# One encoder layer in fp32 on one core: attention sums kept as channels x tokens up to the output projection, with the group norms applied to partial products

## The chip, the core and the metric

The kernel runs on one core of a Trainium2 chip. The core has a matrix engine (TensorE; PE in the profile, with its weight loads as PEld), a vector engine (VectorE, DVE), a scalar engine (ScalarE, ACT), a general engine (GpSimd, POOL) and a queue for transfers (SyncE, SP). Each engine works through its own instructions in order, and semaphores make one wait for another. On-chip memory (SBUF) has 128 partitions; TensorE writes its results to PSUM, eight banks of 128 x 512 fp32 numbers. The metric is the time of one execution on the device in microseconds (us).

## What is computed

One layer of an encoder for 1024 tokens of 1024 channels, all in fp32 (cut from the reference):

```python
hn = rms_norm(x, norm1_g)
proj = hn @ w_in                       # 1024 x 2304: qA kA vA qB kB vB
qa = axial_rope(rms_norm(qa)); ka = axial_rope(rms_norm(ka))
out_a = softmax(qa @ ka.T / 8) @ va    # 8 query heads, 2 key/value heads, head size 64
out_b = mixture of three dilated windows with ALiBi, merged by their softmax denominators   # 8 heads
mixed = concat([rms_norm(out_a, outa_norm_g), rms_norm(out_b, outb_norm_g)])   # two groups of 512
x = x + mixed @ w_out
x = x + conv_ffn(rms_norm(x, norm2_g)) # up 1024 -> 5632, width-3 conv, gelu gate, down 2816 -> 1024
```

`rms_norm` of a group divides each token's 512 channels by the root of their mean square and multiplies them by a gain.

## The kernel before

**Numbers.** A product of two fp32 matrices is made from three faster products of "high" and "low" parts (tiles in `bigr`): high x high, high x low, low x high. For each operand ScalarE copies the high part and VectorE (sometimes GpSimd) subtracts it from the original to give the low part. Products in plain fp32 (`f(...)` operands) take two passes.

**Stages, in order of time.** (1) The input projection, by a seven-product (Strassen-like) scheme, with the queries, keys and values prepared in its wake; to about 200 us. (2) Mixer A, to 391 us: 16 groups, one for each pair of a 128-token query block `b` and a key/value head `kv`; a group has four query heads x 128 tokens in its 512 columns. For each of eight key tiles `a_main` (line 924) makes 128 keys x 512 queries of scores in a bank, ScalarE takes the exponential twice (once as the high part, once in place in PSUM), VectorE subtracts to give the low part, and three steps later `pv` (line 932) multiplies with the values. The values carry a block of 64 columns of ones, so that the denominators come out under the 64 channels: the bank `ob` (6 or 7, by turns) ends with 64 rows of channels and 64 rows that all hold the denominator. `a_prep` (line 895), spread among these steps, prepares the next group, with eight row maxima on VectorE. (3) Mixer B, to about 541 us: eight heads in eight steps each (`b_s`, `b_prep`, `b_pv`, lines 1073, 1009, 1111), the products with the values two steps behind the scores (`lag = 2`, line 1399). Four steps use high and low parts, four use plain fp32 products with the values `F_VCN`, 65 columns wide (64 channels, one of ones). (4) The output projection, to about 645 us. (5) The up-projection with convolution and gate, to about 1055 us. (6) The down-projection to the end.

**From sums to the projection.** In both mixers the sums lie as channels x tokens when they are done. The kernel turns them: `o_turn` (line 942) in A and `b_out` (line 1135) in B make four PE transposes of 65 rows (64 channels and the denominator), and `o_norm` (line 965) takes the reciprocal of four denominators per partition and multiplies. The result lies as tokens x channels at `q_at(...)`. Then, for each of the eight token tiles and two channel groups, `mix_norm` (line 1165) makes the group norm (square and sum on ScalarE, a root, five small VectorE steps, a pass of 512 with the gain), `mix_tr` (line 1174) turns the tile back with four 128-wide PE transposes and splits it into high and low parts from PSUM, and `proj_out` (line 1183) multiplies with the high and low parts of `w_out` (`wo_split`, line 1145). Both channel groups of a tile accumulate in one bank; `h2_a` (line 1197) adds `x` from there and makes the second norm, `h2_b` (line 1213) turns and splits the result for the up-projection.

**Banks and queues.** Scores, transposes and row maxima take banks in turn from one ring of six (`bank_rings(range(6))`), and from two rings of two in the last head of B and in the projection.

**The order of the work.** The program is recorded first. `Recorder` (lines 126 to 448) finds the dependences, gives each instruction a price (`price`, line 273), simulates the five engines (`simulate`, line 316; PE keeps the order as written, the other engines take what is ready with the earliest due time), and `emit` (line 439) writes the instructions out in the order found. So a price or a delay (`LAG`, line 128) in the planner changes the order on DVE, ACT and POOL and nothing else. In the profile every instruction stands under the one line 447.

**The start.** SyncE and ScalarE issue the first loads (lines 840 to 852): columns 0 to 264 of `w_kv` (8 columns of gain and the first of eight blocks of key/value weights), the first 256 columns of `xt` tile 0, and then the rest. `x_prep` (line 566) splits `xt`, `kv_split` (line 599) scales and splits the weights, `kv_proj` (line 610) is the first work on PE.

Of the kernel before, what the change touches and what calls it, by code (L numbers as in the profile page):

```python
# [123 lines left out]

class Recorder:
# [147 lines left out]
    def price(self, op, outs, ins):  # L273
# [42 lines left out]
    def simulate(self, order=None, window=400):  # L316
# [134 lines left out]
def tile_encoder_layer(ctx, tc, x, xt, w_kv, w_in, gains, outg, norm2_g, w_out, w_up, conv,  # L451
# [472 lines left out]
    def a_main(g, prep, tail, late, plan, late_plan):  # L924
# [14 lines left out]
        def o_out():  # L939
            act(f(F_OT[g % 2], 512)[0:65], bank(ob)[0:65], AF.Copy)  # L940

        def o_turn():
# [20 lines left out]
        return [lambda: pv(5), lambda: pv(6), lambda: pv(7), o_out, o_turn]  # L963

    def o_norm(t, step, dst, dims):
        rec = f(SM_T + 88 + 8 * (t % 2), 4)
        vec.reciprocal(rec, pp(512 * t + 64, [step, 4]))
# [818 lines left out]
```

## Time and profile before

| | |
|---|---|
| median of 3 runs | 1274.68 us (1273.49 to 1274.68) |
| the profiled execution | 1274.05 us |
| its span, first to last instruction | 1272.3 us |
| ScalarE busy in the span | 744.6 us (59%) |
| GpSimd busy in the span | 90.8 us (7%) |
| granted TensorE clock | 1.000 |
| moved by DMA | 157.43 MB |

How to read what follows. The page gives each engine's busy time and a row of 40 digits, one for each fortieth of the span (31.8 us): the busy share in tenths, 9 for 90% and more. The chain that ended last is followed back from the last instruction to whatever released it. A group of instructions stands as: engine, operation, what is written from what (`ps` is PSUM, `bigf` and `bigr` the two arrays in SBUF, with partitions x elements), its count, then its busy time in us and the mean length of one in ns, then the engine's idle time just before them and what ended it. Lengths of neighbours on an engine can overlap, so the busy time of a group can be less than count x mean. The timeline has the start and length of a run of like instructions in us. The view by stretches gives, for A:B in us, the length, and each engine's busy time with its number of instructions.

### The profile page before, as it was taken

Reading aid. Unit: us, or ns where it says so; the run is one execution under the profiler, and the core shown is the slowest. Engines: PE = TensorE matmul, PEld = TensorE weight load, DVE = VectorE, ACT = ScalarE, POOL = GpSimd, SP = SyncE. Lnnn points to the kernel's source line nnn. Section 1 sums busy time; section 2 is a strip of 40 time slices with the busy share of each in tenths; the row PEclk is TensorE's granted clock in tenths of the full one; section 3 lists DMA queues with packets and bytes.
Section 4 is the critical chain, followed back from the end, with each engine's and each line's share of the span. In section 5 each row is a group of like instructions: output and inputs, shape, how many; then the busy total and the mean of one; then the engine's idle time right before and its main releaser. Section 6 shows DMA issues by size and latency. Waiting matters only on the chain.

```text
span 1272.3 us, 17870 instructions
## 1 busy us (share of the span) xinstructions
PE 1258.9 (99%) x6244; PEld 1047.8 (82%) x6244; DVE 1078.3 (85%) x1943; ACT 744.6 (59%) x1221; POOL 90.8 (7%) x92
## 2 busy tenths in 40 slices
PE   8999999999999999999999999999999999999998
PEld 7888877888888998878888888888888888888887
DVE  6998899999887887886699999999999998876664
ACT  7875569988887677763455444444444455343331
POOL 0021230010001221001120000000000000000000
PEclk9999999999999999999999999999999999999999
DMA  9251350000004455342312322223322247967872
GB/s 353 90 164 50 83 145 17 18 1 10 1 18 135 116 121 130 123 151 100 108 59 74 112 105 99 90 103 114 116 104 95 96 161 262 351 224 225 292 228 105
DMA packets 118921, 157.43 MB, mean 124 GB/s; under 512 B 50736, under 2 KB 76336, under 8 KB 117808
## 3 DMA queue, kind: packets, MB, share of 16 engines
q1 hardware_dynamic: 117536, 153.02, 37.2%
q0 software_dynamic: 1152, 3.15, 0.9%
q8 instruction: 49, 0.80, 0.3%
q14 instruction: 40, 0.33, 0.1%
q10 hardware_dynamic: 144, 0.14, 0.0%
HBM read 118.26 MB, written 33.82 MB: 120 GB/s over the span
## 4 chain that ended last, share of the span: by engine, by line
PE 96%; DVE 2%; ACT 1%; DMA 1%; issue 0%; POOL 0%; SPq 0%; ACTq 0%; DVEq 0%
PE ps L447 96%; DVE bigf L447 1%; DVE bigr L447 1%; ACT bigr L447 0%; DMA bigf<-xt 0%; DMA bigf<-w_out 0%; ACT L447 0%; ACT ps L447 0%; POOL bigf L447 0%; ACT bigf L447 0%; SPq L447 0%; ACTq L447 0%; DVEq L447 0%
## 5 line engine op out<-in xcount | busy, mean ns | idle before, releaser
L447 PE MATMUL ps<-bigr 128*128 128x512 f32 (+3 forms) x5860 | 1228.3, 369 | 8.3 <-ACT bigr L447 5.4
L447 PEld LDWEIGHTS ps<-bigr 128*128 128x128 f32 x5860 | 1009.8, 186 | 205.8 <-ACT bigr L447 11.0
L447 ACT ACTIVATE bigr<-bigf 128x512 fp32r<-128x512 f32 (+2 forms) x387 | 277.1, 728 | 355.2 <-PE ps L447 300.0
L447 DVE TENSOR_TENSOR bigr<-bigf,bigr 128x512 fp32r<-128x512 f32 (+2 forms) x355 | 284.7, 812 | 56.5 <-ACT bigr L447 54.8
L447 DVE TENSOR_TENSOR bigf<-bigf 128x512 f32<-128x512 f32 (+3 forms) x308 | 212.6, 712 | 22.1 <-DMA bigf<-w_down 13.1
L447 ACT ACTIVATE bigr<-ps 128x512 fp32r<-128x512 f32 (+1 forms) x292 | 166.4, 602 | 79.5 <-PE ps L447 76.9
L447 DVE TENSOR_TENSOR bigf<-ps,bigf 128x512 f32<-128x512 f32 (+3 forms) x260 | 174.4, 680 | 34.7 <-PE ps L447 30.1
L447 DVE SCALAR_TENSOR_TENSOR bigf<-bigf 128x255 f32<-128x255 f32 (+5 forms) x283 | 165.4, 595 | 21.1 <-ACT bigf L447 18.0
L447 ACT ACTIVATE bigf<-bigf 128x1024 f32<-128x1024 f32 (+5 forms) x194 | 152.1, 804 | 36.1 <-DVE bigf L447 30.4
L447 DVE TENSOR_TENSOR bigr<-ps,bigr 128x512 fp32r<-128x512 f32 x188 | 127.1, 684 | 33.9 <-ACT ps L447 23.9
L447 ACT ACTIVATE ps<-ps 128x512 f32<-128x512 f32 x192 | 115.2, 601 | 9.7 <-PE ps L447 8.9
L447 ACT ACTIVATE bigf<-ps 128x512 f32<-128x512 f32 (+3 forms) x112 | 70.3, 634 | 24.0 <-PE ps L447 12.9
L447 DVE TENSOR_REDUCE bigf<-ps 128x1 f32<-128x512 f32 x128 | 81.2, 680 | 0.8 <-PE ps L447 0.7
L447 POOL TENSOR_TENSOR bigr<-bigf,bigr 128x512 fp32r<-128x512 f32 x32 | 41.9, 1313 | 320.6 <-ACT bigr L447 187.7
L447 PE MATMUL ps<-bigf 128*128 128x128 f32 (+2 forms) x384 | 63.2, 294 | 1.0 <-DVE bigf L447 0.8
L447 PEld LDWEIGHTS ps<-bigf 128*128 128x128 f32 (+2 forms) x384 | 43.2, 139 | 14.3 <-DVE bigf L447 2.3
L447 POOL TENSOR_TENSOR bigf<-bigf 128x256 f32<-128x256 f32 (+2 forms) x29 | 36.2, 1269 | 184.2 <-DVE bigf L447 90.2
L447 DVE CUSTOM_DVE_ANT_1 bigf<-ps,bigf 128x432 bf16<-128x432 f32 x64 | 38.6, 603 | 3.4 <-PE ps L447 3.2
L447 DVE CUSTOM_DVE_ANT_0 bigf<-ps,bigf 128x256 bf16<-128x256 f32 x64 | 26.8, 419 | 2.3 <-PE ps L447 1.3
L447 DVE TENSOR_REDUCE bigf<-bigf 128x16 f32<-128x1024 f32 x13 | 15.8, 1215 | 1.1 <-ACT bigf L447 1.1
L447 ACT ACT_TABLE_LOAD x11 | 14.1, 1283 | 4.0 <-DVE bigf L447 2.6
L447 POOL MEMSET bigr<- 64x512 f32 (+2 forms) x18 | 8.2, 477 | 49.5 <-PE ps L447 49.4
(17 smaller groups left out, 51.8 us busy)
## 6 DMA issues: line engine op xcount, KB each, us to landing
bigf<-w_down SPq DMA_DIRECT2D x99, 256.0 KB, 3.8
bigf<-w_up SPq DMA_DIRECT2D x44, 512.0 KB, 3.4
bigf<-gscr SPq DMA_DIRECT2D x77, 256.0 KB, 4.0
gscr<-bigf SPq DMA_DIRECT2D x33, 512.0 KB, 3.2
bigf<-w_in SPq DMA_DIRECT2D x8, 1024.0 KB, 7.1
bigf<-x SPq DMA_DIRECT2D x16, 512.0 KB, 4.5
bigf<-tmx SPq DMA_DIRECT2D x8, 672.0 KB, 4.1
bigr<-bigr SPq DMA_DIRECT2D x16, 256.0 KB, 3.1
```

Source lines behind the costliest of these rows:

```text
L447: method(*args, **kw)
```

## The change

- **No turning.** The values of B (`F_VCN`) get 64 columns of ones, so that B too ends with 64 rows of denominators. `o_out` in A and `b_out` in B take the reciprocal of these rows (256 elements twice per group in A, 512 for each half head in B) and multiply. The result stays channels x tokens, two heads one under the other in a tile of 128 partitions. `o_turn`, `o_norm`, `mix_norm` and `mix_tr` go.
- **Norms.** Squares are summed over channels: GpSimd (and in the last head ScalarE and VectorE) squares the results and adds them up in `F_SS`; `square_sums` turns these sums with four PE transposes for each half of the tokens and group, and VectorE adds over the partitions' remaining 128 channels. `mix_rms` makes all eight tiles' roots of a group at once. The gain is multiplied into `w_out` in `wo_split`. Each channel group now has a bank of its own in the projection; `proj_add` scales it by the token's root and adds it to `x`.
- **Low parts.** In A the low parts of key tiles 0 and 4 are made by GpSimd; the second exponential goes to SBUF for these.
- **Start.** The first loads are twice as wide (rows of 2 KB); tile 3 of `xt` also comes in halves and joins the first half products.
- **Planner.** Some prices and delays change; `MOVES` is empty and adds nothing.

The diff, cut to its core:

```diff
-    LAG = ((215, 200, 200, 200, 195), (150, 150, 140, 185, 157), (135, 122, 140, 168, 115), (150, 150, 150, 150, 80))
+    LAG = ((215, 200, 200, 200, 195), (166, 150, 146, 185, 157), (142, 124, 140, 168, 115), (150, 150, 150, 150, 80))
...
+            t = n / 1.2 + (52 if ps(ins[0]) else 94) + (37 if ps(outs[0]) else 0)
...
+                t += 12
+            if name == "reciprocal":
+                t += 24
...
+            late_weights = 105 if e == 0 and c[0] < 200 and t > free[0] + 20 else 0
+            free[e] = t + c[0] + late_weights
...
-    act_dma(f(F_WC - 8, 264), w_kv[:, 0:264])
-    dma(f(qab(0), 256), xt[0][:, 0:256])
-    kv_load(1, 2)
+    act_dma(f(F_WC - 8, 520), w_kv[:, 0:520])
+    dma(f(qab(0) + 0, 512), xt[0][:, 0:512])
     kv_load(2, 4)
...
         def o_out():
-            act(f(F_OT[g % 2], 512)[0:65], bank(ob)[0:65], AF.Copy)
-
-        def o_turn():
-            t = next_tr()
-            for i in range(4):
-                pe.transpose(bank(t, 65, 128 * i), f(F_OT[g % 2] + 128 * i, 128)[0:65], f(O_IDF, 65)[0:65])
-            o_norm(t, 128, q_at(1, b, kv), ([64, 4], [1, 64]))
+            o, d = F_OT[g % 2], F_OT[g % 2] + 256
+            for u in range(2):
+                rows = slice(64 * u, 64 * u + 64)
+                ps = pp(512 * ob + 128 * u, [256, 2], [1, 128])
+                act(fp(o, [128, 2], [1, 128])[rows], ps[0:64], AF.Copy)
+                vec.reciprocal(fp(d, [128, 2], [1, 128])[rows], ps[64:128])
+            gp.tensor_tensor(f(q_at(1, b, kv), 256), f(o, 256), f(d, 256), op=OP.mult)
+            if kv:
+                o = fp(q_at(1, b, 0), [512, 2], [1, 256])
+                gp.tensor_tensor(heads(f(F_SQ, 512), 2), o, o, op=OP.mult)
+                gp.tensor_tensor(f(F_SQ, 256), f(F_SQ, 256), f(F_SQ + 256, 256), op=OP.add)
+                gp.tensor_tensor(f(F_SS + 128 * b, 128), f(F_SQ, 128), f(F_SQ + 128, 128), op=OP.add)
...
-            act(bank(st), bank(st), AF.Exp)
-            vec.tensor_tensor(r(pl, 512), bank(st), rf(ph, 512), op=OP.subtract)
+            if kt in (0, 4):
+                act(f(p, 512), bank(st), AF.Exp)
+                gp.tensor_tensor(r(pl, 512), f(p, 512), rf(ph, 512), op=OP.subtract)
+            else:
+                act(bank(st), bank(st), AF.Exp)
+                vec.tensor_tensor(r(pl, 512), bank(st), rf(ph, 512), op=OP.subtract)
...
+    def square_sums(u, hf):
+        t = next_tr()
+        for i in range(4):
+            tr_f(t, i, f(F_SS + 512 * hf + 128 * i, 128))
+        vec.tensor_reduce(f(F_RMS + 8 * u + 4 * hf, 4), heads(bank(t), 4), axis=AX.X, op=OP.add)
...
-                mm(bank(6 + rr // 2, 256, 256 * (rr % 2))[0:65], f(F_VCN + 66 * (2 * rr + 1 - u), 65),
+                mm(bank(6 + rr // 2, 256, 256 * (rr % 2)), f(F_VCN + 128 * (2 * rr + 1 - u), 128),
...
-            o = f(F_OS + 512 * hf, 512)
-            vec.tensor_tensor(o[0:65], bank(6 + hf)[0:65], o[0:65], op=OP.add)
+            vec.tensor_tensor(f(F_OD, 512), bank(6 + hf), f(F_OS + 512 * hf, 512), op=OP.add)
+            b_out(h, hf)
 
     def b_out(h, hf):
-        t = next_tr()
-        for i in range(4):
-            pe.transpose(bank(t, 65, 128 * i), f(F_OS + 512 * hf + 128 * i, 128)[0:65], f(O_IDF, 65)[0:65])
-        o_norm(t, 128, q_at(0, 4 * hf, h // 4) + 64 * (h % 4), ([1024, 4], [1, 64]))
+        o, d = f(F_OD, 512), f(F_RD, 512)
+        x = fp(q_at(0, 4 * hf, h // 4) + 128 * (h % 4 // 2), [1024, 4], [1, 128])
+        vec.reciprocal(d[0:64], o[64:128])
+        if h % 2 == 0:
+            gp.tensor_tensor(x[0:64], heads(o[0:64], 4), heads(d[0:64], 4), op=OP.mult)
+            return
+        vec.tensor_tensor(x[64:128], heads(o[0:64], 4), heads(d[0:64], 4), op=OP.mult)
+        sq, ss = f(F_SQ, 512), f(F_SS + 512 * hf, 512)
+        if h == 1:
+            gp.tensor_tensor(heads(ss, 4), x, x, op=OP.mult)
+        elif h < 7:
+            gp.tensor_tensor(heads(sq, 4), x, x, op=OP.mult)
+            gp.tensor_tensor(ss, ss, sq, op=OP.add)
+        else:
+            act(heads(sq, 4), x, AF.Square)
+            vec.tensor_tensor(ss, ss, sq, op=OP.add)
...
+    def mix_rms(u):
+        s, v, rt, t = [f(F_RMS + 16 * i + 8 * u, 8) for i in range(4)]
+        vec.tensor_scalar(v, s, 1.0 / 512, EPS, op0=OP.mult, op1=OP.add)
+        act(rt, v, AF.Sqrt)
+        newton(s, v, rt, t)
+
+    def mix_split(i, u):
+        o, d = fp(q_at(1 - u, seq(i), 0), [512, 2], [1, 256]), xs(i) + 512 * u
+        act(heads(r(d, 512), 2), o, AF.Copy)
+        vec.tensor_tensor(heads(r(d + 1024, 512), 2), o, heads(rf(d, 512), 2), op=OP.subtract)
...
+    def proj_add(i, u, hf):
+        x = f(F_X + 1024 * (i % 2) + 512 * hf, 512)
+        vec.scalar_tensor_tensor(f(qab(seq(i)) + 512 * hf, 512) if u else x, bank(pj(i, u, hf)),
+                                 f(F_RMS + 8 * u + seq(i), 1), x, op0=OP.mult, op1=OP.add)
...
-    mix_norm(0, 1)
-    mix_norm(1, 1)
-    mix_tr(0, 1)
+    mix_split(0, 1)
+    proj(1, 0, 0)
+    square_sums(1, 0)
+    proj(1, 0, 1)
+    square_sums(1, 1)
+    mix_rms(1)
+    mix_split(1, 1)
```

More of the change, by code (lines that the diff above doesn't have):

```diff
@@ L1 @@
+import random
 from contextlib import ExitStack
@@ L329, in lag @@
             if eng[i] == eng[j]:
-                return 120 if self.short[i] else 0
+                return 120 if self.short[i] or self.ops[i][1] == "tensor_tensor_reduce" else 0
             return self.LAG[eng[i]][eng[j]] + (100 if eng[i] == 2 and not eng[j] and self.short[i] else 0)
@@ L437, in simulate, with emit @@
         return seq, max(free)
-    def emit(self, tc):
+    def emit(self, tc, moves=()):
         self.edges()
+        self.off = [0.0] * len(self.ops)
+        for seed, at, width, sigma, share in moves:
+            rng = random.Random(seed)
+            for i in range(max(0, at - width), min(len(self.ops), at + width)):
+                if self.ops[i][0] in (1, 2, 3) and self.ops[i][1] != "dma_start" and rng.random() < share:
+                    self.off[i] += rng.gauss(0, sigma)
         order, _ = self.simulate()
@@ L961, in a_main @@
                 pv(kt - 3)
[L963 to L967, printed above, removed]
-        vec.tensor_tensor(fp(dst, *dims), pp(512 * t, [step, 4], [1, 64]), rec[:, :, None].to_broadcast([128, 4, 64]),
-                          op=OP.mult)
+        return [lambda: pv(5), lambda: pv(6), lambda: pv(7), o_out]
+    def square_sums(u, hf):
[3 more added lines that the diff above has]
+        vec.tensor_reduce(f(F_RMS + 8 * u + 4 * hf, 4), heads(bank(t), 4), axis=AX.X, op=OP.add)
     def nat_rows(h, t):
@@ L1163, in x_load, with pj, proj @@
         dma(f(F_X + 1024 * (i % 2), 1024), perm_rows(x, seq(i), D))
[L1165 to L1184 removed]
+    def mix_rms(u):
[7 more added lines that the diff above has]
+        vec.tensor_tensor(heads(r(d + 1024, 512), 2), o, heads(rf(d, 512), 2), op=OP.subtract)
+    def pj(i, u, hf):
+        return (0, 1, 2, 3, 6, 7)[pj_at.setdefault((i, u, hf), len(pj_at)) % 6]
+    pj_at = {}
+    def proj(i, u, hf):
+        b = pj(i, u, hf)
         for k in range(4 * u, 4 * u + 4):
@@ L1200, in h2_a @@
         for hf in range(2):
-            vec.tensor_tensor(f(o + 512 * hf, 512), bank(pj(i, hf)),
-                              f(F_X + 1024 * (i % 2) + 512 * hf, 512), op=OP.add)
+            proj_add(i, 1, hf)
         act(f(hn(i), 1024), f(o, 1024), AF.Square, accum_out=f(t, 1))
@@ L1264, in tile_encoder_layer @@
             kv_proj(2, (0,))
-        for half in range(i + 1 < 3, 2):
+            kv_proj(3, (0,))
+        for half in range(i + 1 < 4, 2):
             x_prep(i + 1, half)
-        kv_proj(i, (1,) if i < 3 else (0, 1))
+        kv_proj(i, (1,) if i < 4 else (0, 1))
         kv_out(i)
@@ L1388, in mixer_out_early @@
                 wo_load(k)
-        if s in (0, 1):
-            mix_norm(s, 0)
+        if s == 2:
+            mix_rms(0)
         if s in (1, 3):
-            mix_tr(s // 2, 0)
+            mix_split(s // 2, 0)
         if s >= 4:
-            wo_split(s - 4, vec.tensor_copy)
+            wo_split(s - 4, True)
         if s == 7:
-            proj_out(0, 0, 0)
-            proj_out(0, 0, 1)
+            proj(0, 0, 0)
+            proj(0, 0, 1)
     lag = 2
@@ L1417, in tile_encoder_layer @@
                 load_vc(h1 + 1)
-        h1, s1 = divmod(gs - lag - 1, 8)
-        if h1 >= 0 and s1 in (5, 7):
-            b_out(h1, (s1 - 5) // 2)
+        if gs == 8:
+            square_sums(0, 1)
         if s == 7 and h < 6:
```

102 lines of the change are left out of this document (48 added, 54 removed).

## The prediction

> **What bounds the kernel now.** I read the page first: busy shares, slices, chain.
>
> ```profile
> span 1272.3 us, 17870 instructions
> PE 1258.9 (99%) x6244; PEld 1047.8 (82%) x6244; DVE 1078.3 (85%) x1943; ACT 744.6 (59%) x1221; POOL 90.8 (7%) x92
> PE   8999999999999999999999999999999999999998
> DVE  6998899999887887886699999999999998876664
> PE 96%; DVE 2%; ACT 1%; DMA 1%; issue 0%; POOL 0%; SPq 0%; ACTq 0%; DVEq 0%
> ```
>
> TensorE (PE) is busy in 99% of the span and carries 96% of the chain that ended last. So each PE instruction that goes is time won, as long as nothing else becomes late. But the VectorE (DVE) row also stands at 8 and 9 through the attention slices: the room in which DVE may grow is small. I therefore took the attention stages alone, with the view of busy time by stretches. Its columns: length, PE busy (count), PEld, DVE, ACT, POOL, clock, DMA share, GB/s.
>
> ```profile
> 209.80:294.80 85.00, 84.98 (x420) 67.87 (x419) 81.55 (x152) 76.78 (x150) 9.62 (x4) 1.00 0.05 10
> 294.80:367.00 72.20, 72.20 (x360) 58.34 (x359) 64.26 (x120) 62.46 (x119) 0.00 (x0) 1.00 0.00 1
> 367.00:391.00 24.00, 24.00 (x146) 20.12 (x146) 18.64 (x57) 19.75 (x38) 3.88 (x3) 1.00 0.23 60
> 427.68:446.35 18.67, 18.67 (x141) 16.77 (x140) 15.08 (x49) 13.65 (x26) 4.38 (x4) 1.00 0.51 131
> 391.00:546.70 155.70, 153.68 (x1108) 135.64 (x1106) 127.58 (x383) 115.78 (x209) 27.55 (x25) 1.00 0.49 131
> ```
>
> The first three rows are mixer A: 7, 6 and 2 of its 16 groups, about 12.1 us each. The fourth is one head of mixer B, the fifth all of mixer B with the way into the output projection. DVE works 81.55 of 85.00 us in the first seven groups (96%), 64.26 of 72.20 in the next six, 15.08 of 18.67 in a head.
>
> **PE: what goes and comes.** Each group and each half head ends in four PE transposes of 65 columns; 32 such sets go. The PE rows in order of time (start, length, what, count) show what a set costs, and four 128-wide ones likewise:
>
> ```profile
> 211.25 0.39 PE L447 MATMUL ps<-bigr 128*128 128x512 f32 x1
> 211.48 0.41 PE L447 MATMUL ps<-bigf 65*128 65x65 f32 x4
> 211.69 0.48 PE L447 MATMUL ps<-bigr 128*128 128x512 f32 x1
> 580.66 1.03 PE L447 MATMUL ps<-bigf 128*128 128x128 f32 x8
> 581.45 6.53 PE L447 MATMUL ps<-bigr 128*128 128x512 f32 x27
> ```
>
> From 211.48 to 211.69 a set takes 0.21 us, and the matmul behind it lasts 0.48 where its like before lasts 0.39: 0.30 us a set, 32 x 0.30 = 9.6 us. Eight 128-wide ones take 0.79 us, so 0.40 a set plus half of that 0.09: 0.44. The 16 sets of mix_tr go (7.0 us), the four of square_sums come (1.8 us). PE loses 9.6 + 7.0 - 1.8 = 14.8 us of work. The mixer B products with 128 instead of 65 columns keep their number and their 256 moving columns; their weight loads cost the same:
>
> ```profile
> L447 PEld LDWEIGHTS ps<-bigf 128*65 128x65 f32 x128 | 16.1, 137 | 5.1
> L447 PEld LDWEIGHTS ps<-bigf 128*128 128x128 f32 x128 | 15.1, 140 | 4.9 <-DVE bigf L447 2.3
> ```
>
> **DVE: the reciprocals become wide.** This is the step on which I stake the forecast. Before, tokens lie on partitions and a reciprocal has four elements per partition. Left as channels x tokens, the denominators lie along the free axis: two reciprocals of 256 elements for each A group (32), one of 512 for each half head (16). No row is that wide, but there are four widths to extend (mean ns behind the busy time):
>
> ```profile
> L447 DVE RECIPROCAL bigf<-bigf 128x1 f32<-128x1 f32 x24 | 3.6, 157 | 2.8 <-ACT bigf L447 2.8
> L447 DVE RECIPROCAL bigf<-bigf 128x8 f32<-128x8 f32 x1 | 0.2, 185 | 0.0
> L447 DVE RECIPROCAL bigf<-bigf 128x16 f32<-128x16 f32 x9 | 2.1, 240 | 0.2 <-ACT bigf L447 0.2
> L447 DVE RECIPROCAL bigf<-bigf 128x64 f32<-128x64 f32 x1 | 0.5, 543 | 0.0
> L447 DVE TENSOR_TENSOR bigf<-bigf 128x64 f32<-128x64 f32 x2 | 0.4, 222 | 0.0
> ```
>
> From 16 to 64 elements a reciprocal grows by 303 ns in 48 elements, 6.3 ns each; from 1 to 64 by 386 in 63, 6.1. A tensor_tensor of the same 64 takes 222, not 543. With 6.2 ns, 256 elements take 543 + 192 x 6.2 = 1.73 us and 512 take 543 + 448 x 6.2 = 3.32 us. Bounds: at about one element per ns, as other DVE operations run, 0.36 and 0.63 us, which is what the planner's new price says (n/0.96 + 68 + 24 ns); upward 6.9 ns each, the steepest pair (185 to 240 ns in eight elements), 1.87 and 3.63 us. I take 6.2, the slope up to the row nearest in width. [...]
>
> **Mixer A.** The DVE timeline of one group gives what goes (start to next start, since neighbours overlap by about 0.08 us):
>
> ```profile
> 333.03 0.68 DVE L447 TENSOR_TENSOR bigr<-ps,bigr 128x512 fp32r<-128x512 f32 x1
> 333.63 0.15 DVE L447 TENSOR_REDUCE bigr<-bigf 128x4 fp32r<-128x8 f32 x1
> 333.70 0.17 DVE L447 RECIPROCAL bigf<-ps 128x4 f32<-128x4 f32 x1
> 333.91 0.43 DVE L447 TENSOR_TENSOR bigf<-ps,bigf 128x256 f32<-128x256 f32 x1
> 334.25 1.28 DVE L447 TENSOR_TENSOR bigr<-ps,bigr 128x512 fp32r<-128x512 f32 x2
> ```
>
> A low part costs 0.60 (333.03 to 333.63), and two of eight go to GpSimd: -1.20. Reciprocal and scaling of o_norm go: 333.70 to 334.25, -0.55. Two reciprocals come: 2 x 1.65 = +3.30. Together +1.55 us a group. First seven: 81.55 + 10.85 = 92.4 us of DVE in what were 85.0, so +7.4. Next six: 64.26 + 9.3 = 73.6 against 72.2, +1.4. The last two reach 18.64 + 3.1 = 21.7, below PE's 24.0 - 0.6: -0.6. That is +8.2 with DVE never idle; waits between DVE, ACT and PE leave it 0.1 to 0.4 us per group now, so I add 1.8: **+10 us**. The transposes won there (16 x 0.30) are then no gain, since DVE sets the pace. With the late work spread evenly over all groups it is 164.45 + 15 x 1.55 = 187.7 for 181.2, +6.5; with much unevenness +16.
>
> What waits behind a reciprocal: the low parts of the next exponentials and the row maxima, and for them PE's probability-value products three steps on and its score banks. GpSimd has room for its two low parts and products (1.31 us and about 1 us each, from these rows) in a 12 us group; ACT's one copy of the sums becomes two of 0.38 us for one of 0.59, unseen beside 10.4 us.
>
> ```profile
> L447 POOL TENSOR_TENSOR bigr<-bigf,bigr 128x512 fp32r<-128x512 f32 x32 | 41.9, 1313 | 320.6 <-ACT bigr L447 187.7
> L447 POOL TENSOR_TENSOR bigf<-bigf 128x256 f32<-128x256 f32 x20 | 18.5, 958 | 27.9 <-ACT bigf L447 18.3 <-DVE bigf L447 8.7 <-ACT bigr L447 1.0
> L447 ACT ACTIVATE bigf<-ps 65x512 f32<-65x512 f32 x16 | 9.5, 594 | 3.2 <-PE ps L447 2.8
> L447 ACT ACTIVATE bigf<-ps 128x256 f32<-128x256 f32 x8 | 2.8, 378 | 3.2 <-PE ps L447 3.1
> ```
>
> **Mixer B.** In 391.0 to 546.7 DVE works 127.58 us. To it come 16 x 3.24 = 51.8 (reciprocals), 10 x 0.60 = 6.0 (the odd heads' products, two sums); out go 16 x 0.55 = 8.8 (o_norm) and about 3.8 (three mix_norm, less one mix_rms). That makes 172.8 us of DVE for 155.7: +17.1 with DVE never idle. It will idle: both reciprocals of a head fall within two or three of its eight steps of 2.33 us, which makes 6.5 us of DVE in a lump, while PE is only two steps ahead and turns six score banks. In a steady head DVE rests 18.67 - 15.08 = 3.6 us now, 28 us over the stage; that a fifth of it stays unused is +5. **+22 us**; from +15 (rest used up, gaps closed) to +32.
>
> **Output projection, start, rest.** Behind 546.7 PE is busy without a break and DVE far from it:
>
> ```profile
> 575.00:600.00 25.00, 25.00 (x127) 20.46 (x126) 17.40 (x43) 8.51 (x18) 2.60 (x2) 1.00 0.32 106
> 725.00:750.00 25.00, 25.00 (x112) 20.70 (x111) 23.73 (x37) 10.70 (x16) 0.00 (x0) 1.00 0.23 74
> ```
>
> So there the PE work counts: 13 of the 16 mix_tr sets (5.7 us) less two of square_sums (0.9): **-4.8 us**. The doubled proj_add (16 more of about 0.7 us on DVE) takes the place of the norms' 1.5 us each; the 17.40 of 25 hides it. Cover gone, it would cost at most 16 x 0.7 = 11. The up-projection keeps all its instructions; only queue order may shift there: 0. At the start PE waits till 5.02 us:
>
> ```profile
> 5.02 2.04 PE L447 MATMUL ps<-bigr 128*128 128x256 f32 x6 [5.02 <-ACT bigr L447]
> 7.00 0.42 ACT L447 ACTIVATE bigr<-bigf 128x256 fp32r<-128x256 f32 x1 [1.40 <-DMA bigf<-xt]
> 0.00:25.00 25.00, 19.55 (x122) 18.47 (x123) 14.54 (x30) 15.74 (x29) 0.21 (x4) 1.00 0.92 340
> ```
>
> The first two transfers become twice as large, 256 KB more at 340 GB/s is 0.8 us later; in return ACT's later wait of 1.40 us for the second half goes. Between -0.8 and +0.8: 0.
>
> **The sum**, against the profiled execution's own 1274.05 us (1.75 above its span, 0.6 below the median 1274.68): 1274.05 + 10 + 22 - 4.8 = **1301 us**, 2.1% slower. A difference of 0.2% (2.5 us) is about what a measurement can tell here.
>
> **Rivals.** (1) Faster: a wide reciprocal runs at one element per cycle. Then A's DVE work falls by 1.75 - 0.72 = 1.03 us a group, a head's stays near 15 + 0.8, nothing but PE binds, and the time is 1274.05 - 14.8 = 1259. It decides at B: 15.08 + 0.6 - 1.1 + 2R must stay under 18.67 - 0.6, so R under 1.75 us for 512 elements, 3.4 ns each. For it: only the planner's price. Against it: four rows on one line, at nearly twice the limit. 0.11. (2) Wide reciprocals cost a third more per element than the 6.2 ns of the narrow ones: 32 x 0.40 = 13 and 16 x 0.93 = 15 us more, 1329. No pair of rows is that steep, but none is as wide. 0.06. [...] (3) Each reciprocal stops PE for its whole length since the queue order is planned for 0.36 and 0.63 us: A 16 x (3.30 - 0.30) = 48, B 16 x (3.24 - 0.30) = 47, 1274 + 95 - 4.8 = 1364. Six banks and the lag of three steps in A speak against the whole of it, the lumps in B for a part. 0.08. (4) PE runs on beside it all, DVE's lateness absorbed so far that the lost and won parts cancel, 1274 within 2.5. It needs 25 us more idle DVE than the rows show. 0.05.
>
> **How the numbers follow.** My forecast has 0.70 and spreads from 1285 (A +6.5, B +15, projection and stalls -7, start -1) to 1324 (A +16, B +32, -4, with GpSimd work in the way). The range reaches up over rival 2 and the near part of rival 3's time, and a little down for gaps that close better: 1280 to 1335. Left out are rival 1, rival 4 and half of rival 3. Slower 0.84 (forecast, 2 and 3), faster 0.13 (rival 1 and the lower edge of 4), same 0.03.
>
> **What would show it.** The changed profile should have 32 reciprocals of 256 with a mean near 1.7 us and 16 of 512 near 3.3; DVE at 9 through slices 6 to 16; PE idle, or in short waits, there, put down to DVE; A some 10 us longer, B some 22; the projection 5 shorter, with PE unbroken; the up-projection unchanged at 112 matmuls per 25 us. Reciprocals of 0.4 and 0.7 us would prove me wrong altogether; right durations with A and B at their old length would mean that the idle DVE time was larger or better used than the rows say.

## The result, and the profile after

The changed kernel takes 1335.95 us (median of 5 runs, 1335.73 to 1336.51); the kernel before took 1273.87 us in the runs beside it. The ratio is 1.0489, with a 95% interval of 1.0476 to 1.0501: 62 us slower, where 27 were forecast, and 1 us above the range. The direction and the cause were foreseen; the size was not.

The page of the changed kernel, the lines that answer to those shown of before:

```profile
span 1334.7 us, 17513 instructions
PE 1265.8 (95%) x6068; PEld 1052.1 (79%) x6068; DVE 1161.5 (87%) x1836; ACT 739.7 (55%) x1192; POOL 182.4 (14%) x182
PE   8999998889998888888999999999999999999998
DVE  6988889999998989899769999999999999876664
PEclk9999999999998999889999999999999999999999
PE 59%; DVE 5%; issue 2%; ACT 1%; POOL 1%; DMA 0%; ACTq 0%; DVEq 0%; POOLq 0%
```

PE, unbroken before, falls to 8 in the slices of mixers A and B (7 to 9 and 13 to 19), and its share of the chain falls from 96% to 59%. The granted clock stands at 8 in three of these slices (13, 17 and 18), where the kernel before had 9 throughout. There are 176 matmuls fewer (6068 for 6244) and yet more PE busy time (1265.8 for 1258.9).

Now the stages. I cut both traces at the starts of the first score product of A, the first product of B and the first of the up-projection, and at B's last plain fp32 product with the values. The view by stretches gives A, B, output projection and rest, first of the kernel before, then of the changed one (columns: length, PE, PEld, DVE, ACT, POOL busy with counts, clock, DMA share, GB/s):

```profile
189.70:387.20 197.50, 196.98 (x983) 157.93 (x982) 181.00 (x353) 175.98 (x334) 16.35 (x12) 1.00 0.06 13
387.20:542.00 154.80, 152.85 (x1116) 135.54 (x1115) 125.47 (x377) 113.15 (x204) 27.55 (x25) 1.00 0.48 127
542.00:638.30 96.30, 96.20 (x477) 78.25 (x476) 71.29 (x184) 47.45 (x112) 10.05 (x8) 1.00 0.35 118
638.30:1267.90 629.60, 629.58 (x2783) 520.88 (x2781) 537.47 (x760) 277.13 (x353) 6.56 (x5) 1.00 0.44 151
```

```profile
189.20:410.10 220.90, 200.81 (x927) 154.18 (x926) 213.17 (x324) 180.97 (x349) 83.40 (x78) 0.99 0.05 11
410.10:603.40 193.30, 160.89 (x1049) 147.84 (x1048) 171.56 (x355) 114.87 (x204) 53.70 (x49) 0.91 0.38 106
603.40:700.80 97.40, 92.28 (x427) 74.69 (x425) 76.40 (x131) 36.20 (x67) 9.57 (x8) 0.98 0.35 111
700.80:1330.30 629.50, 629.47 (x2783) 520.90 (x2780) 540.26 (x760) 277.29 (x353) 6.83 (x5) 1.00 0.44 151
```

A is 23.4 us longer (+10 forecast), B 38.5 (+22 forecast), the projection 1.1 longer (4.8 shorter forecast). Start (189.7 and 189.2) and rest (629.6 and 629.5) do not move, as forecast. In A, DVE works 213.2 of 220.9 us, and PE's 20.0 us of waiting there all end with DVE: it sets the pace. In B it works 171.6 of 193.3, which leaves 21.7 us unused although the stage grew.

The reciprocals themselves came out nearly as extrapolated (1.73 and 3.32 us). Groups of DVE by shape, changed kernel, mean ns behind the busy time:

```profile
L466 DVE RECIPROCAL bigf<-ps 64x256 f32<-64x256 f32 x32 | 56.3, 1760 | 0.9
L466 DVE RECIPROCAL bigf<-bigf 64x512 f32<-64x512 f32 x16 | 53.6, 3348 | 0.5
```

What they cost in place is more. Timeline of DVE in A, changed kernel (start, length, what, count):

```profile
319.12 0.69 DVE L466 TENSOR_TENSOR bigr<-ps,bigr 128x512 fp32r<-128x512 f32 x1
319.73 1.28 DVE L466 TENSOR_REDUCE bigf<-ps 128x1 f32<-128x512 f32 x2
...
326.75 0.69 DVE L466 TENSOR_TENSOR bigr<-ps,bigr 128x512 fp32r<-128x512 f32 x1
327.48 1.76 DVE L466 RECIPROCAL bigf<-ps 64x256 f32<-64x256 f32 x1
329.26 0.69 DVE L466 TENSOR_TENSOR bigr<-ps,bigr 128x512 fp32r<-128x512 f32 x1
329.99 1.76 DVE L466 RECIPROCAL bigf<-ps 64x256 f32<-64x256 f32 x1
331.78 0.43 DVE L466 TENSOR_TENSOR bigr<-bigf,bigr 128x256 fp32r<-128x256 f32 x1
```

A low part followed by a row maximum takes 0.61 us from start to start (319.12 to 319.73), overlapped by 0.08. Followed by a reciprocal it takes 0.73 (326.75 to 327.48, 329.26 to 329.99), and the reciprocal takes 1.78 and 1.79 to the next start. Nothing overlaps at either end. So one reciprocal costs 1.79 + (0.73 - 0.61) = 1.91 us, not the 1.65 that I counted by taking the usual overlap off. The reciprocal reads rows 64 to 127 between instructions that read from row 0. None of the changed kernel's 48 wide reciprocals overlaps a neighbour: the gaps on both sides are 0.01 to 0.04 us. Nor does a product of 64x512 with its output from row 64 on (606.48 to 607.17, the next starts at 607.20). Two of the runs below speak for the rows, and not the reciprocal, as the reason. In e1_copy_all a multiplication with the same rows (427 ns on average) stands in its place, and the low part ahead of it again takes 0.73 us (305.86 to 306.59). In e7_packed_a the reciprocal starts at row 0, and it overlaps its neighbours:

```profile
322.70 1.75 DVE L466 RECIPROCAL bigf<-bigf 128x256 f32<-128x256 f32 x1
324.36 0.63 DVE L466 TENSOR_TENSOR bigr<-ps,bigr 128x512 fp32r<-128x512 f32 x1
```

From start to start it takes 1.66 us there, as I had counted. But it also reads SBUF there and not PSUM, so no run changes the rows alone.

Second, GpSimd, twice as busy now, holds DVE up. Timeline of both, changed kernel, and the group of the DVE operation, whose mean was 416 ns before:

```profile
247.96 1.28 POOL L466 TENSOR_TENSOR bigr<-bigf,bigr 128x512 fp32r<-128x512 f32 x1
248.05 1.47 DVE L466 TENSOR_TENSOR bigr<-bigf,bigr 128x256 fp32r<-128x256 f32 x1
```

```profile
L466 DVE TENSOR_TENSOR bigr<-bigf,bigr 128x256 fp32r<-128x256 f32 x16 | 8.7, 546 | 0.3
```

The DVE operation with two inputs in SBUF takes 1.47 us beside a GpSimd low part and ends 0.28 us after it. Three of the 16 are stretched in this way (0.76, 1.47 and 0.97 us), the others take 0.42 to 0.45. A low part that reads PSUM keeps its 0.68 us beside GpSimd (320.92, with GpSimd at work from 320.75 to 322.05). In sum it is small: 16 x 130 ns = 2.1 us for this group, and as much again for four operations of 128x1024 in A with both inputs in SBUF (1744 ns on average, 1216 before).

Third, four reciprocals come in a row at the join of A and B. Timelines of DVE and of PE there, changed kernel (in brackets idle time and who ended it):

```profile
410.49 7.10 DVE L466 RECIPROCAL bigf<-ps 64x256 f32<-64x256 f32 x4
417.63 0.69 DVE L466 TENSOR_TENSOR bigr<-bigf,bigr 128x512 fp32r<-128x512 f32 x1
```

```profile
419.13 0.79 PE L466 MATMUL ps<-bigr 128*128 128x256 f32 x2 [5.07 <-ACT bigr L466]
...
609.14 1.12 PE L466 MATMUL ps<-bigf 128*128 128x128 f32 x4 [2.61 <-DVE bigf L466]
...
615.77 0.66 PE L466 MATMUL ps<-bigf 128*128 128x128 f32 x4 [1.71 <-DVE bigf L466]
```

PE stands still for 5.07 us at the join. In e2_copy_a, where A's reciprocals are short, it waits at most 0.84 us there. The prediction counted these four reciprocals in A, and by its sum they cost nothing; by the stage bounds above they lie in B. The two later rows are the projection's start: `square_sums` waits there for the last head's divisions.

### The profile page after: what moved, and what is told of

Its sections match the earlier page's. It is cut to its first block, busy times and chain, and to the rows that moved or that the text cites. A ratio compares the mean times of both kernels' runs of the same rounds, so it can differ in the third digit from the quotient of the medians.

```text
span 1334.7 us, 17513 instructions
## 1 busy us (share of the span) xinstructions
PE 1265.8 (95%) x6068; PEld 1052.1 (79%) x6068; DVE 1161.5 (87%) x1836; ACT 739.7 (55%) x1192; POOL 182.4 (14%) x182
## 4 chain that ended last, share of the span: by engine, by line
PE 59%; DVE 5%; issue 2%; ACT 1%; POOL 1%; DMA 0%; ACTq 0%; DVEq 0%; POOLq 0%
PE ps L466 59%; DVE bigf L466 4%; DVE bigr L466 1%; ACT bigr L466 1%; POOL bigf L466 0%; POOL bigr L466 0%; ACT ps L466 0%; DMA bigf<-w_out 0%; ACT bigf L466 0%; ACTq L466 0%; DVEq L466 0%; POOLq L466 0%
## 5 line engine op out<-in xcount | busy, mean ns | idle before, releaser
L466 ACT ACTIVATE bigr<-ps 128x512 fp32r<-128x512 f32 x276 | 158.6, 598 | 111.0 <-PE ps L466 107.9
L466 DVE TENSOR_TENSOR bigf<-ps,bigf 128x512 f32<-128x512 f32 (+1 forms) x212 | 151.0, 720 | 29.1 <-PE ps L466 22.6
L466 DVE SCALAR_TENSOR_TENSOR bigf<-bigf 128x255 f32<-128x255 f32 (+4 forms) x239 | 145.6, 632 | 5.1 <-ACT bigf L466 2.8
L466 POOL TENSOR_TENSOR bigf<-bigf 128x256 f32<-128x256 f32 (+4 forms) x87 | 87.0, 1008 | 250.2 <-DVE bigf L466 235.5
L466 POOL TENSOR_TENSOR bigr<-bigf,bigr 128x512 fp32r<-128x512 f32 x64 | 83.0, 1302 | 230.2 <-ACT bigr L466 135.5
L466 ACT ACTIVATE bigf<-ps 128x512 f32<-128x512 f32 (+3 forms) x160 | 91.8, 579 | 34.6 <-DVE bigf L466 14.3
L466 DVE TENSOR_REDUCE bigf<-ps 128x1 f32<-128x512 f32 (+1 forms) x132 | 84.2, 680 | 1.9 <-PE ps L466 1.8
L466 DVE RECIPROCAL bigf<-bigf 64x512 f32<-64x512 f32 (+4 forms) x37 | 57.7, 1568 | 2.3 <-ACT bigf L466 1.7
L466 DVE RECIPROCAL bigf<-ps 64x256 f32<-64x256 f32 x32 | 56.3, 1760 | 0.9
L466 PE MATMUL ps<-bigf 128*128 128x256 f32 (+1 forms) x208 | 46.8, 350 | 5.4 <-DVE bigf L466 5.4
L466 PEld LDWEIGHTS ps<-bigf 128*128 128x128 f32 x208 | 31.7, 172 | 10.4 <-DVE bigf L466 6.7
L466 DVE SCALAR_TENSOR_TENSOR bigf<-ps,bigf 128x512 f32<-128x512 f32 x32 | 23.5, 747 | 9.4 <-PE ps L466 6.1
```

The lines of the kernel that those rows point to most:

```text
L466: method(*args, **kw)
```

## The experiments

The table has the stage lengths in us of each kernel's profiled execution, by the same cuts, and the median times. The profiled execution of e4_priced was 3.2 us below its median and that of e9_narrow_a_pairs 2.3 us above, the others within 1.2. The rest is 629.3 to 629.6 in all but e9_narrow_a_pairs (630.8).

| kernel | A begins | A | B | projection | time |
|---|---|---|---|---|---|
| before | 189.7 | 197.5 | 154.8 | 96.3 | 1273.87 |
| changed | 189.2 | 220.9 | 193.3 | 97.4 | 1335.95 |
| e1_copy_all | 189.8 | 192.1 | 147.3 | 92.9 | 1257.43 |
| e2_copy_a | 188.8 | 192.2 | 187.4 | 97.4 | 1301.36 |
| e3_copy_b | 189.5 | 220.9 | 152.9 | 93.6 | 1291.48 |
| e4_priced | 192.8 | 208.4 | 189.1 | 94.2 | 1323.30 |
| e5_low_dve | 189.0 | 233.1 | 194.8 | 97.4 | 1351.03 |
| e6_narrow | 188.7 | 194.0 | 186.0 | 100.2 | 1305.40 |
| e7_packed_a | 188.2 | 197.6 | 191.4 | 97.4 | 1310.52 |
| e8_pairs | 195.1 | 194.5 | 160.5 | 94.8 | 1279.69 |
| e9_narrow_a_pairs | 193.9 | 192.2 | 172.2 | 94.8 | 1287.78 |
| e10_wide_price | 188.7 | 196.1 | 160.5 | 94.5 | 1275.39 |
| e11_wo_act | 189.0 | 196.1 | 158.4 | 93.1 | 1272.39 |
| e12_low_pool | 189.1 | 196.1 | 156.1 | 94.2 | 1270.74 |

**e1_copy_all, e2_copy_a, e3_copy_b.** The reciprocals become multiplications by one (427 and 554 ns on average for 256 and 512 columns), of the same shapes and in the same order: everywhere, in A alone, in B alone. So these three leave the softmax division out.

```diff
-                vec.reciprocal(fp(d, [128, 2], [1, 128])[rows], ps[64:128])
+                rec.ops.append((2, "reciprocal", nc.vector.tensor_scalar, (fp(d, [128, 2], [1, 128])[rows], ps[64:128], 1.0, None), {"op0": OP.mult}))
...
-        vec.reciprocal(d[0:64], o[64:128])
+        rec.ops.append((2, "reciprocal", nc.vector.tensor_scalar, (d[0:64], o[64:128], 1.0, None), {"op0": OP.mult}))
```

> The changed kernel with all 48 wide reciprocals replaced by a copy of the same rows (a multiplication by 1.0), in the same queue order. It leaves the reciprocals out, so the softmax division is not done. Theory D (the wide reciprocals make DVE the bound in both mixers): mixer A back from 221 to about 193 us, mixer B from 193 to about 150, the projection some 5 us under the 96 of before; 1260 us, between 1255 and 1270. Rival G (GpSimd's extra work, and its holding up of DVE operations with two SBUF inputs, is the larger part): these stay, so 1300 or more. Rival P (the queue order, planned for short reciprocals, is what costs) also gives about 1260 here and is told apart by the priced variant.

> Only mixer A's 32 reciprocals of 256 are replaced by copies (mixer A's division is left out); mixer B keeps its 16 of 512. Theory D: mixer A falls from 221 to about 193 us, mixer B stays at 193; 1308 us. If the stages add up, this and the variant with copies in B alone together account for the whole difference of the variant without any. Rival G: above 1325.

> Only mixer B's 16 reciprocals of 512 are replaced by copies (mixer B's division is left out); mixer A keeps its 32 of 256. Theory D: mixer B falls from 193 to about 150 us and the wait at the beginning of the projection goes (some 6 us), mixer A stays at 221; 1287 us, between 1282 and 1293. Rival G: above 1315.

Measured: 1257.43 us (ratio 0.9865, 0.9849 to 0.9882), 1301.36 (1.0215, 1.0199 to 1.0230) and 1291.48 (1.0134, 1.0119 to 1.0149). The whole loss, and 16 us more, hangs on the length of these 48 instructions. The two stages add up: 34.6 + 44.5 = 79.1 us for one at a time, 78.5 for both. In e2_copy_a B falls as well, from 193.3 to 187.4 us, where 193 was expected: the stop at the join with A goes. Stretches A and B of e1_copy_all:

```profile
189.80:381.90 192.10, 191.69 (x927) 155.13 (x926) 173.80 (x324) 180.31 (x349) 84.61 (x78) 1.00 0.05 12
381.90:529.20 147.30, 144.87 (x1048) 135.38 (x1047) 129.06 (x357) 114.07 (x206) 54.04 (x49) 1.00 0.51 139
```

PE is full again in A (191.69 of 192.10) with as many GpSimd instructions as in the changed kernel, so GpSimd's new work does not carry the loss. Compare PE's busy time in B for the same work: 144.9 us here at a clock of 1.00, 160.9 in the changed kernel at 0.91 (160.9 x 0.91 = 146). So the lower clock accounts for most of PE's extra busy time in B; how much of B's length it accounts for is not shown.

**e4_priced.** The planner gets a price near the measured one; no instruction changes, only the order.

```diff
-                t += 24
+                t += 5.2 * n + 100
```

> The changed kernel with the planner's price of a reciprocal set to what the profile shows (5.2 ns more per element and 0.1 us): the same instructions in another queue order. Theory D, with a bound by the amount of DVE work: mixer A has 13.1 us of DVE in a late group and cannot fall under about 213 us, mixer B 21.1 of 23.6 us in a head, so at best about 175; 1310 to 1328 us. Rival P (the order is what costs): under 1295.

Measured: 1323.30 us (1.0380, 1.0364 to 1.0395). By the medians, the order made with the wrong price is worth 12.7 of the 62 us. Stretch A of e4_priced:

```profile
192.80:401.20 208.40, 199.41 (x927) 153.63 (x926) 202.25 (x320) 178.58 (x349) 78.37 (x76) 0.99 0.04 10
```

In the profiled executions A is 12.5 us shorter, B 4.2 and the projection 3.2, and A begins 3.6 us later, of which more below. DVE's busy time in A falls from 213.2 to 202.3. The hold-ups beside GpSimd are among what goes: within A the group of 128x256 shown above falls from a mean of 564 ns to 424. Another part has only moved: four DVE operations fewer lie in A (x320 for x324).

**e5_low_dve.** The two low parts per group go back from GpSimd to VectorE.

```diff
-            if kt in (0, 4):
+            if kt in ():
```

> The changed kernel with all low parts of mixer A back on DVE (two more of eight per group; GpSimd keeps its products and squares). Theory D: DVE is the bound in mixer A, so 16 x 2 x 0.60 us = 19 us longer, less some 4 us in which DVE operations with two SBUF inputs stood behind GpSimd's low parts; 1351 us. Rival G (GpSimd is the cause): shorter than the 1336 of the changed kernel.

Measured: 1351.03 us (1.0605, 1.0589 to 1.0621). Stretch A of e5_low_dve:

```profile
189.00:422.10 233.10, 204.54 (x922) 157.50 (x922) 225.37 (x346) 178.56 (x347) 45.48 (x47) 0.97 0.04 10
```

DVE's busy time in A grows by 12.2 us (213.2 to 225.4), and A grows by 12.2. In A each us of DVE work is a us of time; in e4_priced it is nearly so downward (10.9 of work, 12.5 of time). Were GpSimd's work the cause, less of it would have made the kernel shorter; it is 15.1 us longer.

**e6_narrow.** The denominators of both mixers go to DRAM as one row, come back as 128 partitions x 4, are inverted there, and come back spread over 64 partitions.

```diff
+    def inverse(i, row, *outs):
...
+        four = f(F_D4 + 4 * (i % 4), 4)
+        dma(at(dscr, 0, [512, 1], [1, 512]), row)
+        dma(four, at(dscr, 0, [4, 128], [1, 4]))
+        vec.reciprocal(four, four)
+        dma(at(iscr, 0, [4, 128], [1, 4]), four)
+        for dst, o, ap in outs:
+            dma(dst, at(iscr, o, [0, 64], *ap))
```

> The changed kernel with narrow reciprocals: the 512 denominators of a group (A) or half head (B; the last head keeps its wide ones) go through a DRAM row into a tile of 128 partitions x 4, one reciprocal of four elements per partition is taken, and the result comes back from DRAM, read for 64 partitions at once. All is computed. DVE loses 28 x about 3.5 us; five or four small transfers of about 2 us each come, in a chain of about 10 us that nobody waits for before the next group but one. Theory D: PE is the bound again in both mixers; 1274 - 15 and some exposed latency, 1260 us, between 1256 and 1272, faster than the kernel before. Rival G: 1300 or more. If the transfers hold up the queue or GpSimd, between the two.

Measured: 1305.40 us (1.0250, 1.0235 to 1.0265): a miss by 45 us. A is as hoped (194.0), B is not (186.0). Its row and the waits of the whole run (who waits for what, us, times, longest):

```profile
382.70:568.70 186.00, 157.04 (x1048) 143.75 (x1047) 125.30 (x361) 112.86 (x203) 54.66 (x51) 0.93 0.48 117
```

```profile
POOL bigf L467 <- DMA bigr<-iscr: 47.4, 7, 17.6
...
POOL bigf L467 <- DMA bigf<-iscr: 34.4, 12, 8.8
```

DVE has only 125.3 us of work in B, as before the change, and B is long all the same: GpSimd waits up to 17.6 us for an inverted row, DVE 8.4 us for B's first table, and SyncE's queue 28.1 us over the whole run (20 waits) for the transfers out before it issues those back. This is the third case of the expectation, transfers that hold up the queue or GpSimd. The run speaks neither for nor against the amount of DVE work in B.

**e7_packed_a.** In A, ScalarE copies both halves' denominators one under the other, and one reciprocal of 128 partitions x 256 does for two of 64 x 256.

```diff
-                vec.reciprocal(fp(d, [128, 2], [1, 128])[rows], ps[64:128])
+                act(fp(d, [128, 2], [1, 128])[rows], ps[64:128], AF.Copy)
+            vec.reciprocal(f(d, 256), f(d, 256))
             gp.tensor_tensor(f(q_at(1, b, kv), 256), f(o, 256), f(d, 256), op=OP.mult)
```

> The changed kernel with mixer A's two reciprocals of 64 partitions x 256 per group made into one of 128 partitions x 256: ScalarE copies the denominators below one another into the 128 rows, then one reciprocal follows. Theory D with a cost per column and none per partition: DVE loses 1.9 us per group and mixer A falls from 221 to about 200 to 205 us (ScalarE gets 0.76 us more per group and is near full in the first groups); 1318 us. If 128 partitions cost twice what 64 do: 1336 as before.

Measured: 1310.52 us (1.0297, 1.0279 to 1.0314), 7 better than expected. Groups by shape, e7_packed_a:

```profile
L466 DVE RECIPROCAL bigf<-bigf 128x256 f32<-128x256 f32 x16 | 27.8, 1741 | 0.7 <-ACT bigf L466 0.7
```

Twice the partitions take 1741 ns where 64 took 1760 (read from PSUM): the cost goes by columns alone. With both in SBUF e8_pairs shows the same, 3348 ns for 128 x 512 as for 64 x 512 above. With half the reciprocals A is back at 197.6 us.

**e8_pairs and e9_narrow_a_pairs.** The same thought in B: the sums of two neighbouring heads share one reciprocal of 128 x 512. e8 packs A as e7 does, e9 takes A from e6. Both have the planner's higher price. The diff shows the lines of B alone.

```diff
-            vec.tensor_tensor(f(F_OD, 512), bank(6 + hf), f(F_OS + 512 * hf, 512), op=OP.add)
+            vec.tensor_tensor(f(F_RD[hf], 512)[rows], bank(6 + hf)[64:128], o[64:128], op=OP.add)
+            vec.tensor_tensor(x[rows], heads(bank(6 + hf)[0:64], 4), heads(o[0:64], 4), op=OP.add)
...
-        vec.reciprocal(d[0:64], o[64:128])
         if h % 2 == 0:
-            gp.tensor_tensor(x[0:64], heads(o[0:64], 4), heads(d[0:64], 4), op=OP.mult)
             return
-        vec.tensor_tensor(x[64:128], heads(o[0:64], 4), heads(d[0:64], 4), op=OP.mult)
+        vec.reciprocal(d, d)
+        (gp if h < 7 else vec).tensor_tensor(x, x, heads(d, 4), op=OP.mult)
```

> Keeps the whole change, but divides less often on VectorE: in A one reciprocal of 128 partitions x 256 per group, as before in e7 (ScalarE copies the denominators of both halves beside each other); in B the sums of two neighbouring heads go straight to their places in the channels x tokens tile, their denominators to rows 0-63 and 64-127 of one tile, and one reciprocal of 128 x 512 and one 128-row multiply by GpSimd serve both heads; the planner has the reciprocal's measured price. VectorE's work per head and half in B: the two adds of 64 rows (0.6 us each) and half a reciprocal (1.7) against one add, one reciprocal (3.35) and half a multiply: 2.8 us less per head, 18.3 instead of 21.1. Theory (the loss is the amount of VectorE's work in each stage): A 197 us; B at 18.3 of work plus the 2.5 idle of a head is 20.8 x 8 = 166 plus its ends, so 165 to 172 against 193.3; the time 1283 to 1292. Rival (the loss in B comes with the wait of the next step for each division, whatever VectorE's share): a reciprocal on 128 rows waits for the second head, so half of e3's 40 us, B near 173, but with A's join and the projection's start not better: the time 1290 to 1300.

> As e8_pairs, but in A the denominators go through DRAM to a tile of 128 partitions x 4, are inverted there and come back spread over 64 partitions, as in e6 (A took 194.0 us there); B divides by pairs of heads with no transfer. Theory (amount of VectorE's work): A 193 to 195, B as in e8_pairs, 165 to 172; the time 1279 to 1288, and the SP queue's waits for the inverted rows that held B up in e6 are gone. Rival (the round trip costs B through the queue whichever stage issues it): B stays near e6's 186, the time near 1300.

Measured: 1279.69 us (1.0049, 1.0037 to 1.0062) and 1287.78 (1.0111, 1.0096 to 1.0127). Stretch B of e8_pairs:

```profile
389.60:550.10 160.50, 151.93 (x1057) 139.82 (x1056) 149.58 (x356) 116.62 (x207) 54.50 (x51) 0.99 0.47 130
```

DVE has 22 us less work in B than in the changed kernel and B is 33 us shorter, below the 165 to 172 expected: with DVE's work below PE's, most of PE's waiting goes (8.6 us for 32.4), and with it the low clock (0.99). The time of e9 is at the upper edge of what the theory gave, 1279 to 1288; its rival, the round trip through the queue, shows at one place. Waits of e9_narrow_a_pairs from 386 to 426 us:

```profile
DVE bigf L466 <- DMA bigf<-tmx: 9.3, 1, 9.3
...
PE ps L466 <- DVE bigf L466: 8.8, 2, 8.5
```

The load of a table that B needs first is issued behind A's last inverted rows, and PE stands for 8.5 us. That is most of the 11.7 us by which B is longer than in e8.

**e10_wide_price and e11_wo_act.** e10 is e8 with the higher price for wide reciprocals only; e11 also lets ScalarE make four high halves of the output weights in the last head of B.

```diff
-                t += 24
+                t += 24 if n < 256 else 5.2 * n + 100
...
-            wo_split(s - 4, True)
+            wo_split(s - 4)
```

> e8_pairs with the planner's higher price of a reciprocal kept for those of 256 elements and more; the narrow ones of the norms in the start are priced as in the change. In e8 A began at 195.1 us against 189.2 of the changed kernel, in e4 at 192.8. Theory (the higher price put the narrow reciprocals of the start in a worse order): A begins at 189 to 190, A, B and projection as in e8 (194.5, 160.5, 94.8), the time 1274 to 1276. Rival (the start is late for another reason, such as the norms' own order around the first group): A still begins near 195 and the time stays 1279 to 1281.

> As e10_wide_price, and the high halves of the first output-projection weights, which VectorE makes in the last head of B, are made by ScalarE (busy 10 to 17 of 25 us there in e8, VectorE 24 of 25): 4 operations of 128x1024 less on VectorE, some 4 us. Theory (VectorE's amount of work sets the end of B too: PE busy 23.4 of 25 at 525 to 550 us and 21.2 of 25 at 550 to 575 in e8): 3 to 5 us less than e10, 1269 to 1273, so at or under the kernel before. Rival (the end of B waits for the chain of the last two divisions, not for VectorE's amount): within 1.5 us of e10.

Measured: 1275.39 us (1.0013, 1.0004 to 1.0021) and 1272.39 (0.9992, 0.9983 to 1.0001). A begins at 188.7 again, so the late start of e4 and e8 came from the price of the narrow reciprocals; A itself is 1.6 longer than in e8, B the same. A stretch at the start of the projection, shortly behind the end of B, first in e10, then in e11:

```profile
550.00:575.00 25.00, 21.80 (x90) 17.14 (x91) 23.84 (x45) 8.89 (x15) 0.00 (x0) 0.86 0.40 126
```

```profile
550.00:575.00 25.00, 23.49 (x104) 17.54 (x105) 23.41 (x44) 10.25 (x18) 0.00 (x0) 1.00 0.45 146
```

With four wide operations less on DVE, PE does 14 matmuls more in these 25 us and keeps its full clock; B is 2.1 us shorter, the projection 1.4. The time falls by 3.0 us, the low edge of what was expected; by its interval e11 is not told from the kernel before.

**e12_low_pool.** As e11; in B too GpSimd makes some low parts, two of the four in each head.

```diff
-        act(bank(st), bank(st), AF.Exp)
-        if s < 4:
+        low = s in (0, 2)
+        act(f(p, 512) if low else bank(st), bank(st), AF.Exp)
+        if low:
+            gp.tensor_tensor(r(pl, 512), f(p, 512), rf(ph, 512), op=OP.subtract)
+        elif s < 4:
             vec.tensor_tensor(r(pl, 512), bank(st), rf(ph, 512), op=OP.subtract)
```

> As e11_wo_act, and two of the four low parts of each head of B (steps 0 and 2) are subtracted by GpSimd from an exponential that ScalarE writes to SBUF, as the change does with two of eight in A: 2 x 0.67 us less on VectorE per head, which is busy 24.2 of 25 us there in e11; GpSimd takes 1.3 us for one. Theory (VectorE's amount of work sets B): VectorE falls to about 22.5 of 25, B from 158.4 to 150 to 154, the time 1264 to 1269, under the kernel before by more than the measurement is uncertain. Rival (B now waits on each pair's reciprocals, which run in twos, whatever VectorE's share): B stays within 2 us of 158.4 and the time at 1271 to 1274.

Measured: 1270.74 us (0.9976, 0.9967 to 0.9985): 0.24% under the kernel before, and of the versions that keep the division the one that beats both by more than the measurement is uncertain. Stretch B of e12_low_pool:

```profile
385.20:541.30 156.10, 149.94 (x1048) 138.17 (x1047) 140.92 (x340) 117.83 (x210) 74.81 (x65) 0.98 0.51 133
```

B is longer than the 150 to 154 us expected. It has 8.1 us of DVE work less than in e11 (149.0 there) and is 2.3 us shorter: DVE's work no longer sets this stage alone, and the rival came nearer than the theory. What binds B now (the join with A, where PE works 21.2 us of the 25 from 375 to 400, is one candidate) was not tried.

## Why the prediction was right in kind and short in size

**Reciprocal's length: right.** 1.76 and 3.35 us against 1.73 and 3.32. The slope of 6.2 ns per element, read off four narrow rows, holds to eight times their width; rivals 1 and 2 fall with it.

**Where the 35 us are.** The forecast fell short by 16.5 us in B, 13.4 in A and 5.9 in the projection.

**PE's term: right within 2 us.** e1_copy_all, with the division's cost gone, is 16.7 us faster than before; 14.8 were worked out. Stage by stage, A gains 5.4, B 7.5 and the projection 3.4.

**Mixer A, +10 against +23.4: the term that was mis-sized is what a reciprocal takes on DVE's clock.** The prediction took "start to next start, since neighbours overlap by about 0.08 us" and so 1.65. It measured 1.91: 28 of the 32 reciprocals lie in the stretch, and 28 x 0.26 is 7.3 us. The hold-ups beside GpSimd add some 4.2 us (2.1 in the group shown and 2.1 in that of 128x1024). "With DVE never idle" plus 1.8 was short as well: DVE rests 7.7 us of the 220.9, 4.1 of them in waits and the rest in gaps such as those beside the reciprocals. And the last two groups, at "-0.6" in the sum, are the ones whose four reciprocals stop PE at the join. The form of the argument held: in A the stage is DVE's work plus some 6 to 8 us (7.7 here, 6.2 in e4_priced, 7.7 in e5_low_dve).

**The planner's price: seen, and not costed.** The prediction quoted the price of 0.36 and 0.63 us, used it for rivals 1 and 3 alone and gave the forecast nothing for it. e4_priced puts it at 12.7 us, a fifth of the loss.

**Mixer B, +22 against +38.5: the step that failed is "that a fifth of it stays unused is +5".** The DVE work came out near, 172.8 us forecast and 171.6 measured, but in part by luck: the measured stretch has four of A's reciprocals in it (7.0 us) and lacks nearly all of the last head's two (6.4). A steady head of the changed kernel, from the view by stretches:

```profile
482.40:505.90 23.50, 19.54 (x133) 18.10 (x133) 21.58 (x48) 13.95 (x26) 6.74 (x6) 0.93 0.38 96
```

Its 21.6 us of DVE are about what the prediction's own terms make with the measured length (15.08 + 0.6 - 1.1 + 2 x 3.35 = 21.3). But the head lasts 23.5, so 1.9 us stay idle here and 21.7 over the stage, not 5. PE's waits in B of the changed kernel (who waits for what, us, times, longest):

```profile
PE ps L466 <- DVE bigf L466: 12.1, 7, 2.1
PE ps L466 <- ACT ps L466: 10.3, 6, 1.7
PE ps L466 <- ACT bigr L466: 5.3, 2, 5.1
PE ps L466 <- DVE bigr L466: 4.7, 5, 3.8
```

That is 32.4 us, 16.8 of them put down to DVE, and the 5.3 hold the stop at the join. DVE for its part waits 9.0 us for PE and 5.8 for ScalarE, which in turn waits mostly for PE. So each engine stands for the other in turn, and the clock stands at 0.93 in this head. It was 1.00 in all four stretches of before and is 0.91 over this stage, with PE idle for 32.4 us; in B of e9_narrow_a_pairs it was 0.95 (18.0 us idle), of e8_pairs 0.99 (8.6), of e1_copy_all 1.00 (2.4). The amount of waiting alone does not give it: in A PE waits 20.0 us, never more than 2.0 at once, and the clock is 0.99. What lowers it was not shown. How the 16.7 us (21.7 less 5) divide between lumps of two reciprocals and the slower PE was not separated. It is shown that both shrink when DVE's work does (e3_copy_b, e8_pairs).

**Projection, -4.8 against +1.1.** "PE is busy without a break" was read off the kernel before, and the change put two `square_sums`, which need the last head's divisions, at that very place. PE's work did fall, from 96.2 to 92.3 us; the 2.61 and 1.71 us of waiting shown above and some shorter ones ate it up. In e3_copy_b the projection is 93.6.

**Start and rest: right.** Both within 0.5 us.

**The other rivals.** Rival 3, each reciprocal stopping PE for its whole length, would have given 95 us over both mixers; 62 came. In B its 47 us lie nearer to the 38.5 than the forecast's 22, but its reason, the queue order, does not hold there: with the price mended (e4_priced) B is still 189.1 us. In A PE waits 20.0 us beside 49 us of reciprocals. The lumps in B, which the prediction itself named, deserved more than +5. Rival 2's 1329 us lies near the measured time by accident: no run shows its third more per element, and the reciprocals took 1.76 and 3.35 us, 6.2 to 6.3 ns a column. Rival 4, PE running on beside it all, falls with the lengths of A and B.

## What to carry to other kernels

Before a layout is changed to save transposes, count the columns of each slow operation in the new layout: here the division went from 4 columns to 256 and 512, and 512 columns took 3.35 us on 64 partitions and on 128, so two results belong one under the other before they are divided. Where an engine is at nine tenths of a stage, cost its new work without overlap at either end, as the reciprocals of rows 64 to 127 had none here (1.91 us where 1.65 was counted), and add for the stage the stalls of the engine that it feeds. A planner's wrong price is a cost of its own, and here one line mended it.

## What the runs showed of the hardware

- A reciprocal on VectorE grows by 6.2 to 6.3 ns with each column from 64 to 512, on 64 partitions as on 128: 543 ns for 128 x 64, 1741 for 128 x 256, 3348 for 64 x 512 and for 128 x 512.
- The changed kernel's reciprocals of rows 64 to 127 did not overlap their neighbours: 0.73 us from start to start in place of 0.61 for the low part ahead of one, and 0.73 ahead of a copy of the same rows in e1_copy_all. The reciprocal of 128 x 256 that starts at row 0 in e7_packed_a did: 1.66 us from start to start at a length of 1.75.
- A VectorE operation with both inputs in SBUF took 1.47 us beside a GpSimd operation of 1.28, where its like took 0.42 on average before; a low part that reads PSUM took 0.68 beside one of 1.30.
- The same thousand matmuls of B were 144.9 us of busy time at a clock of 1.00 (PE idle for 2.4 us) and 160.9 at 0.91 (idle for 32.4). In A, with 20.0 us of waits of at most 2.0 each, the clock was 0.99.
